# A hybrid trunk layer on one Trainium2 core: 32 of 256 tokens computed from gathered expert rows, the other 224 on the dense expert grid with both parts in one moving operand

## Chip, core and metric

The kernel runs on one core of one Trainium2 chip. A core has TensorE (matmuls, PE in the rows; PEld is its weight load), VectorE (DVE), ScalarE (ACT), GpSimd (POOL) and SyncE (SP, which issues DMAs). The metric is the device time of one execution in microseconds (us), lower is better; a median over several runs is given.

## What is computed

The input is 256 tokens of 2048 channels. The first half of the layer (a sliding-window attention, an mLSTM, a gated merge and an output projection) is untouched by the change. The second half is an expert mixer (PEER), cut here to its core:

```python
qp = (xt @ w_peer_q).reshape(T, 8, 2, 128)                 # 8 heads, two half queries
scores = einsum('thcd,hcnd->thcn', qp, peer_keys)          # against 128 keys each
s_top, i_top = top_k(scores, 16)
cand = s_top[:, :, 0, :, None] + s_top[:, :, 1, None, :]    # 16 x 16 pairs
top_s, pos = top_k(cand, 16);  idx = i0 * 128 + i1          # 16 experts of 16384, per head
gates = softmax(top_s)
act = gelu(einsum('td,thkd->thk', xb, peer_u[idx]))         # 128 rows of u per token
out = einsum('thk,thkd->td', gates * act, peer_v[idx])      # 128 rows of v per token
x = x + out
```

So a token needs 128 of the 16,384 expert rows of `peer_u` and of `peer_v` (2048 channels each).

## The kernel before

Tokens number T = 256, in NT = 2 tiles of 128; channels are 16 tiles of 128 (KT). The kernel does not gather. It streams all of `u` and all of `v` (128 blocks of 128 experts, called i) through TensorE for all tokens, and puts the gates as zeros and non-zeros into a grid `W[i]` (128 experts x 256 tokens, 128 of them; `wA` holds the first 80, `wB` the rest).

A **unit** is one `load` of 128 x 1024 fp32 weights (512 KB, SP's queue, four `raw` buffers) and its `split`: ScalarE copies `raw` to `hi` (L84, rounded to fp32r), VectorE writes `lo = raw - hi` (L85). Each product is then three fp32r matmuls: hi weights by hi and by lo of the activations, lo weights by hi. `hi` and `lo` have two buffers each. `run` prepares unit k+1, then calls `step` for unit k; `step` emits the matmuls, then the functions in `later` (those left by the unit before), then some pieces of the list `side`, as many as the pace `rate` has paid for. What stands in `side` is the work beside the stream: top-16, the lookup, the scatter.

Stages of the second half, in order:
1. `w_pq`, 32 units: query projection; `score` multiplies with the keys, `top16` runs beside it.
2. `u`, 256 units (`ws_units`): a weight block of 128 x 128 is stationary. The hi block moves 512 columns (256 tokens hi, 256 tokens lo, L158), the lo block 256 columns (L162). `total` adds the two halves of the PSUM bank, VectorE multiplies with the norm factor `rb` (L769), ScalarE applies Gelu into `W[i]`. In the first E0 = 52 blocks (104 units) top-16 over pairs (`pick16`), `lookup` (one-hot compare on VectorE, product on GpSimd L807, sum on VectorE) and `turn` run beside; in the other 76 blocks `scatter` does: for four tokens it makes one-hot rows A (VectorE) and B (ScalarE, L847 and L848), multiplies them on TensorE (L853, fp32) and multiplies the result into the blocks that are done (L862) or copies it into those that are not (L864).
3. `v`, 256 units (`v_consume`): here the grid is stationary (`ph`, `pl`, split of `W[i]`) and the weights move, 12 matmuls of 512 columns (L889, L890, L893); the 8 PSUM banks hold 2 token tiles x 2048 channels to the end. Then L904 adds the residual and stores.

The order of each engine's instructions is set by the tile scheduler when the program is built, from the order of the source and its own priorities.

Of the kernel before, what the change touches and what calls it, by code (L numbers as in the profile page):

```python
# [31 lines left out]
QU = 512  # L32


@with_exitstack
def hybrid_block_kernel(ctx: ExitStack, tc: tile.TileContext, a, out):
# [177 lines left out]
    x1d = dram.tile([T, D], F32, name="x1d")  # L214

# [145 lines left out]
    def evac_conv(n):  # L361
        def f(ps):
            total(mqk[:, n], ps)
# [240 lines left out]
    def sig(dst, ps, n):  # L604
        total(dst, ps)
# [14 lines left out]
    def evac_pA(n):  # L620
        def f(ps):
            s = wk.tile([P, T], F32, name="pa", tag="b1", bufs=NB["b1"])
            total(s, ps)
# [3 lines left out]
    def evac_pM(n):  # L627
        def f(ps):
            s = wk.tile([P, T], F32, name="pm", tag="b1", bufs=NB["b1"])
            total(s, ps)  # L630
# [39 lines left out]
    def evac_out(n):  # L670
        def f(ps):
# [15 lines left out]
            split(X2[:, n, 0], X2[:, n, 1], xg)  # L687
            later.append(lambda so=stage["o"]: turn_x1(n, x1, so))
# [13 lines left out]
    iot = exc.tile([P, P], F32, name="iot")  # L702
    G.iota(iot, pattern=[[1, P]], base=0, channel_multiplier=0, allow_small_or_imprecise_dtypes=True)
    gT = exc.tile([P, T], F32, name="gT")
    i0T = exc.tile([P, T], F32, name="i0T")
    i1T = exc.tile([P, T], F32, name="i1T")
    NA = 80
    wA = exc.tile([P, NA, T], F32, name="wA")
    eb = pool(ctx, "eb", 2)

    tks = ExitStack()
    tk = pool(tks, "tk", 1)
    keysT = tk.tile([P, 2 * PH, NK], F32, name="keysT")
# [13 lines left out]
    def score(n, q):  # L727
# [4 lines left out]
        for t in range(NT):  # L732
            side.append(lambda t=t: top16(sc[:, t, n], st_[:, t, n], it_[:, t, n]))

    def evac_q(n):
        def f(ps):
            q = eb.tile([P, T], F32, name="zu")
            total(q, ps)
            V.tensor_mul(q, q, rb)
            later.append(lambda: score(n, q))  # L740
        return f

    units = []
    for n in range(2 * PH):
        units += ws_units(a["w_pq"][n], X2, evac_q(n))
    run(units, 0.75)
    flush()
# [7 lines left out]

    def act_u(i, z):
        k = done["tok"]
        if k < T:
# [208 lines left out]
```

## Time and profile before

| | us |
|---|---|
| median of 3 runs | 2268.75 (2268.66 to 2269.9) |
| the profiled execution | 2268.72 |
| its span from first to last instruction | 2267.0 |
| TensorE busy | 2235.2 (99%) |
| VectorE busy | 1599.0 (71%) |
| ScalarE busy | 1257.8 (55%) |
| GpSimd busy | 85.9 (4%) |

The granted clock over the span is 0.999. The profiled execution lies within 0.1 us of the median, so its span plus 1.7 us outside it stands for the median. The rows below come from this execution. A busy matmul overlaps its neighbours in the records, so a matmul's real cost is read from the distance of starts, not from its duration.

### The profile page before, as it was taken

The numbers are of one execution on the slowest core, as the hardware profiler recorded it, in microseconds if no ns is written. First come the engines' busy times: TensorE is split into PE (matmuls) and PEld (weight loads), VectorE is DVE, ScalarE is ACT, GpSimd is POOL, SyncE is SP. The second block draws the span as 40 slices with busy tenths as digits, with TensorE's granted clock in tenths as the row PEclk, the third lists the DMA queues.
The fourth block names the chain that finished last, engine by engine and source line by source line (L and its number), as shares of the span: only waits on it lengthen the run. The fifth ranks groups of instructions, "written<-read, shape, count | busy, mean of one in ns | idle before, by whom it ended". The sixth has DMA issues, their size and how long they took to land.

```text
span 2267.0 us, 32407 instructions
## 1 busy us (share of the span) xinstructions
PE 2235.2 (99%) x11841; PEld 1906.3 (84%) x11841; DVE 1599.0 (71%) x2915; ACT 1257.8 (55%) x2378; POOL 85.9 (4%) x79
## 2 busy tenths in 40 slices
PE   7999999999999999999999999999999999999999
PEld 5887788888888878888888888888888888888887
DVE  7977688778889997855777788886555555555555
ACT  5755566556544444544777777775444444444443
POOL 3000000000130020200000000000000000000000
PEclk9999999999999999999999999999999999999999
DMA  6565544555665445555544444556555555555555
GB/s 204 189 191 164 169 160 160 184 186 189 211 212 188 162 164 196 181 190 186 171 165 166 165 163 167 165 170 213 195 195 193 193 194 193 194 194 193 194 192 173
DMA packets 115296, 415.66 MB, mean 183 GB/s; under 512 B 12992, under 2 KB 13120, under 8 KB 114752
## 3 DMA queue, kind: packets, MB, share of 16 engines
q1 hardware_dynamic: 115136, 413.59, 55.1%
q8 instruction: 92, 1.51, 0.3%
q14 instruction: 68, 0.56, 0.1%
HBM read 409.35 MB, written 4.19 MB: 182 GB/s over the span
## 4 chain that ended last, share of the span: by engine, by line
PE 91%; DVE 7%; ACT 1%; POOL 1%; issue 0%; DMA 0%; POOLq 0%; SPq 0%; DVEq 0%
PE mm L158 33%; PE mm L162 17%; PE sd L890 5%; PE sd L889 5%; PE mm L889 5%; PE mm L890 5%; PE sd L893 5%; PE mm L893 5%; PE sd L853 3%; DVE lo L85 2%; PE mm L184 2%; PE mm L185 2%; PE mm L189 2%; DVE oh L805 0%; DVE xg L257 0%
## 5 line engine op out<-in xcount | busy, mean ns | idle before, releaser
L85 DVE TENSOR_TENSOR lo<-raw,hi 128x1024 fp32r<-128x1024 f32 x762 | 936.5, 1229 | 611.3 <-ACT hi L84 603.4
L84 ACT ACTIVATE hi<-raw 128x1024 fp32r<-128x1024 f32 x762 | 807.0, 1059 | 863.1 <-PE mm L890 378.5
L158 PE MATMUL mm<-X,hi 128*128 128x512 f32 x3088 | 789.8, 397 | 13.8 <-ACT hi L84 8.5
L158 PEld LDWEIGHTS mm<-X,hi 128*128 128x128 f32 x3088 | 557.4, 190 | 117.7 <-ACT hi L84 8.8
L162 PEld LDWEIGHTS mm<-X,lo 128*128 128x128 f32 x3088 | 421.1, 190 | 39.7 <-DVE lo L85 9.7
L162 PE MATMUL mm<-X,lo 128*128 128x256 f32 x3088 | 433.6, 283 | 5.0 <-DVE lo L85 5.0
L889 PE MATMUL sd<-hi,ph 128*128 128x512 f32 x512 | 199.2, 389 | 0.0
L890 PE MATMUL sd<-hi,pl 128*128 128x512 f32 x512 | 199.2, 389 | 0.0
L890 PE MATMUL mm<-hi,pl 128*128 128x512 f32 x512 | 199.2, 389 | 0.0
L889 PE MATMUL mm<-hi,ph 128*128 128x512 f32 x512 | 199.2, 389 | 0.0
L893 PE MATMUL sd<-lo,ph 128*128 128x512 f32 x512 | 199.2, 389 | 0.0
L893 PE MATMUL mm<-lo,ph 128*128 128x512 f32 x512 | 199.2, 389 | 0.0
L889 PEld LDWEIGHTS mm<-hi,ph 128*128 128x128 f32 x512 | 96.1, 188 | 20.1
L893 PEld LDWEIGHTS sd<-lo,ph 128*128 128x128 f32 x512 | 96.1, 188 | 20.0
L890 PEld LDWEIGHTS mm<-hi,pl 128*128 128x128 f32 x512 | 96.1, 188 | 19.9
L889 PEld LDWEIGHTS sd<-hi,ph 128*128 128x128 f32 x512 | 96.1, 188 | 19.9
L893 PEld LDWEIGHTS mm<-lo,ph 128*128 128x128 f32 x512 | 96.1, 188 | 19.9
L890 PEld LDWEIGHTS sd<-hi,pl 128*128 128x128 f32 x512 | 96.0, 188 | 19.9
L184 PE MATMUL mm<-hi,X 128*128 128x512 f32 x224 | 89.6, 400 | 0.0
L847 ACT ACTIVATE ab<-iot,i1T 128x128 f32<-128x128 f32 x256 | 87.8, 390 | 1.4 <-DVE i1T L823 1.4
L185 PE MATMUL mm<-hi,X 128*128 128x512 f32 x224 | 88.2, 394 | 0.0
L849 DVE TENSOR_SCALAR ab<-iot,i0T,gT 128x128 f32<-128x128 f32 x256 | 74.2, 345 | 0.0
(279 smaller groups left out, 2082.4 us busy)
## 6 DMA issues: line engine op xcount, KB each, us to landing
raw<-u SPq DMA_DIRECT2D x256, 512.0 KB, 3.7
raw<-v SPq DMA_DIRECT2D x256, 512.0 KB, 3.6
raw<-w_g SPq DMA_DIRECT2D x64, 512.0 KB, 3.6
raw<-w_tok SPq DMA_DIRECT2D x56, 512.0 KB, 3.6
raw<-w_qk SPq DMA_DIRECT2D x32, 512.0 KB, 3.7
raw<-w_o SPq DMA_DIRECT2D x32, 512.0 KB, 4.0
raw<-w_pq SPq DMA_DIRECT2D x32, 512.0 KB, 3.7
raw<-w_pa SPq DMA_DIRECT2D x16, 512.0 KB, 3.5
```

The source lines that it names most:

```text
L84: S.activation(hi, src, AF.Copy)
L85: V.tensor_sub(lo, src, hi.bitcast(F32))
L158: PE.matmul(ps, hi[:, w], X[:, k].rearrange("p s t -> p (s t)"), start=(k == 0), stop=False)
L162: PE.matmul(ps[:, :T], lo[:, w], X[:, k, 0], start=False, stop=(k == kts - 1))
L184: PE.matmul(st["ps"][t], xh[:, k, ts], hi[q], start=(k == 0), stop=False)
L185: PE.matmul(st["ps"][t], xl[:, k, ts], hi[q], start=False, stop=False)
L847: S.activation(B, iot, AF.Square, bias=i1T[:, t:t + 1])
L849: V.tensor_scalar(A, iot, i0T[:, t:t + 1], gT[:, t:t + 1], op0=OP.is_equal, op1=OP.mult)
L853: PE.matmul(ps[:, j], AB[j][:, 1], AB[j][:, 0], start=True, stop=True)
L889: PE.matmul(acc[t][h * 2 + q], ph[:, ts], hi[q], start=(i == 0), stop=False)
L890: PE.matmul(acc[t][h * 2 + q], pl[:, ts], hi[q], start=False, stop=False)
L893: PE.matmul(acc[t][h * 2 + q], ph[:, ts], lo[q], start=False, stop=(i == NE - 1))
```

## The change

- **32 tokens leave the grid.** SP = 32, ND = 224: `u_units` and the scatter work on tokens 32 to 255 only. For tokens 0 to 31, `fetch` gathers by an indirect DMA on GpSimd's queue: in one fetch each of the 32 tokens gets one of its 128 expert rows, cut into four quarters of 512 channels on 4 x 32 partitions (128 x 512 fp32, 256 KB), into one of 6 `slab` buffers. `dot` (VectorE, one instruction with an accumulated sum) makes the product with x for u; `add_row` adds weight times row for v. 128 fetches and 128 dots stand in the stream of `u`, 128 fetches and 128 adds in that of `v`, paced by `rows_todo` and `row_rate`.
- **224 tokens move with parts side by side.** In `u` the moving operand is `Xn` (hi and lo of 224 tokens, 448 columns; 224 for the lo weights). `Xn` takes X2's buffer and is made between `w_pq` and `u` by `turn_to_grid` from a copy of the activations that went through DRAM (`xgd`, written from ScalarE's queue by 16 DMAs, read back in one) and was multiplied by `rb` during `w_pq`; so the multiplication per block (L769) goes.
- **The expert sum by column halves.** In `v` the weights become stationary and the grid moves: for each half of the channels, all 128 blocks, 8 matmuls of 448 columns and 8 of 224 into 8 banks; `split_w` makes hi and lo of four blocks at a time into a ring of 8 blocks, which takes `Xn`'s buffer. After each half `total` empties 8 banks. The result is channels x tokens, so `finish` turns it back by 32 transposes at the end.
- **VectorE in source order** from `w_pq` on (`manual_schedule`): the scheduler no longer reorders it. `w_pq` and `u` become one `run`; top-16 of the second token tile moves into `u`; E0 becomes 66; `pick16` looks at 112 pairs instead of 256; `lookup` takes four heads at once (8 GpSimd products of 128 x 1024 instead of 32 of 128 x 256).
- The scatter's A is one VectorE instruction for four tokens; the gate moves from A into B's second ScalarE instruction.

```diff
+SP = 32
+ND = T - SP
+PARTS = P // SP
+HD = D // PARTS
+ROW = 0.75
...
         pace[0] = min(pace[0] + rate, 4.0)
-        while pace[0] >= 1.0 and side:
-            pace[0] -= 1.0
+        if rows_todo:
+            pace[1] += row_rate[0]
+            if pace[1] >= 1.0:
+                pace[1] -= 1.0
+                pace[0] -= ROW
+                rows_todo.pop(0)()
+        while side and pace[0] >= cost(side[0]):
+            pace[0] -= cost(side[0])
             tick()
...
+            def f(parts):
+                Xn = own["Xn"]
...
+                    PE.matmul(ps[:, :2 * ND], hi[:, w], Xn[:, k].rearrange("p s t -> p (s t)"),
+                              start=(k == 0), stop=False)
...
+                    PE.matmul(ps[:, :ND], lo[:, w], Xn[:, k, 0], start=False, stop=(k == KT - 1))
...
+    def turn_to_grid():
+        own["Xn"] = xx.tile([P, KT, 2, ND], F32R, name="X")
+        for c in range(KT // 4):
+            k = slice(4 * c, 4 * c + 4)
+            split(own["Xn"][:, k, 0], own["Xn"][:, k, 1], wA[:, k])
...
+    def fetch(table, s):
+        ix = own["ix"]
+        keep(G.indirect_dma_start(out=slab[s % NSL], out_offset=None, in_=tables[table],
+                                  in_offset=bass.IndirectOffsetOnAxis(ap=ix[:, s:s + 1], axis=0)))
...
+    def dot(s):
+        sl = slab[s % NSL]
+        (V.scalar_tensor_tensor(sl, sl, 1.0, own["x"], op0=OP.mult, op1=OP.mult,
+                                    accum_out=own["dots"][:, s:s + 1]))
+        if s + NSL < NS:
+            fetch("u", s + NSL)
...
+    dve_order = tc.manual_schedule(engines={mybir.EngineType.DVE})
...
+    ue[0] = first(turn_to_grid, ue[0])
+    ue[2] = first(choose, ue[2])
+    run(units + ue, 1.0)
...
+        V.tensor_tensor(A, iot.unsqueeze(1).to_broadcast([P, TG, NK]),
+                        i0T[:, t0:t0 + TG].unsqueeze(2).to_broadcast([P, TG, NK]), op=OP.is_equal)
...
-            S.activation(B, B, AF.Relu, bias=1.0, scale=-1.0)
-            V.tensor_scalar(A, iot, i0T[:, t:t + 1], gT[:, t:t + 1], op0=OP.is_equal, op1=OP.mult)
+            S.activation(B[:, j], B[:, j], AF.Relu, bias=gT[:, t:t + 1], scale=ngT[:, t:t + 1])
...
-                PE.matmul(acc[t][h * 2 + q], ph[:, ts], hi[q], start=(i == 0), stop=False)
-                PE.matmul(acc[t][h * 2 + q], pl[:, ts], hi[q], start=False, stop=False)
...
-                PE.matmul(acc[t][h * 2 + q], ph[:, ts], lo[q], start=False, stop=(i == NE - 1))
...
+            for j in range(NB2):
+                PE.matmul(acc[h][j][:, :2 * ND], hi[:, j * P:(j + 1) * P], both, start=(i == 0), stop=False)
+            for j in range(NB2):
+                PE.matmul(acc[h][j][:, :ND], lo[:, j * P:(j + 1) * P], ring[:, i % NR, 0],
+                          start=False, stop=(i == NE - 1))
+            if i == NE - 1:
+                for j in range(NB2):
+                    total(outT[h][j], acc[h][j][:, :ND], acc[h][j][:, ND:2 * ND])
```

TensorE in the stage `v`, the second half of a unit; `sd` and `mm` are PSUM banks, and of the two names behind the arrow the first moves and the second is stationary (`hi` and `lo` are the weights, `ph` and `pl` the grid, `X` in v the ring). Before:

```order
L889 MATMUL sd<-hi,ph 128x512
L890 MATMUL sd<-hi,pl 128x512
L889 MATMUL mm<-hi,ph 128x512
L890 MATMUL mm<-hi,pl 128x512
L893 MATMUL sd<-lo,ph 128x512
L893 MATMUL mm<-lo,ph 128x512
```

TensorE in the same stage after the change, where one unit ends and the next begins:

```order
L1092 MATMUL sd<-X,lo 128x224
L1092 MATMUL mm<-X,lo 128x224
L1090 MATMUL sd<-X,hi 128x448
L1090 MATMUL mm<-X,hi 128x448
L1090 MATMUL sd<-X,hi 128x448
L1090 MATMUL mm<-X,hi 128x448
```

Twelve matmuls of 512 columns per unit became eight of 448 and eight of 224.

VectorE from `u` into `v` (`zu`, later `z`, is the sum of a block of u, `wB` the grid, `ozt` and `odots` belong to the 32 tokens, `X` is the ring). Before:

```order
L85 TENSOR_TENSOR lo<-raw,hi 128x1024
L199 TENSOR_TENSOR zu<-mm,zu 128x256
L769 TENSOR_TENSOR zu<-zu,rb 128x256
L85 TENSOR_TENSOR lo<-raw,hi 128x1024
L762 TENSOR_TENSOR wB<-wB,zu 128x256
L85 TENSOR_TENSOR lo<-raw,hi 128x1024
L85 TENSOR_TENSOR pl<-wA,ph 128x256
L85 TENSOR_TENSOR lo<-raw,hi 128x1024 x2
```

VectorE at the place where `u` ends, after the change:

```order
L90 TENSOR_TENSOR lo<-raw,hi 128x1024
L215 TENSOR_TENSOR z<-mm,z 128x224
L798 TENSOR_TENSOR wB<-wB,z 128x224
L215 TENSOR_TENSOR z<-mm,z 128x224
L798 TENSOR_TENSOR wB<-wB,z 128x224
L959 TENSOR_TENSOR ozt<-sd,rb 128x32
L961 TENSOR_TENSOR slab_6799<-ozt,gT 128x128
L966 COPY odots<-sd 128x128
L90 TENSOR_TENSOR X<-wA,X 128x4x224
L90 TENSOR_TENSOR lo<-raw,hi 128x1024 x3
```

Before, the `lo` of the first units of v stood between the last pieces of u; now the last blocks of u, the weights of the 32 tokens and the split of the first four grid blocks stand in one row ahead of the first `lo` of v.

VectorE in the scatter stage. Before (`ab` is the pair A and B, `sd` the product on TensorE):

```order
L849 TENSOR_SCALAR ab<-iot,i0T,gT 128x128 x2
L85 TENSOR_TENSOR lo<-raw,hi 128x1024 x2
L199 TENSOR_TENSOR zu<-mm,zu 128x256
L769 TENSOR_TENSOR zu<-zu,rb 128x256
L85 TENSOR_TENSOR lo<-raw,hi 128x1024
L762 TENSOR_TENSOR wB<-wB,zu 128x144
L862 TENSOR_TENSOR wA<-sd,wA 128x4x80
L849 TENSOR_SCALAR ab<-iot,i0T,gT 128x128 x4
```

VectorE in the scatter stage after the change (L949 is the `dot` of a gathered slab):

```order
L90 TENSOR_TENSOR lo<-raw,hi 128x1024
L798 TENSOR_TENSOR wB<-wB,z 128x88
L949 SCALAR_TENSOR_TENSOR slab_6801,odots<-slab_6801,ox 128x512
L1040 TENSOR_TENSOR wA<-sd,wA 128x80x4
L1040 TENSOR_TENSOR wB<-sd,wB 128x9x4
L1040 TENSOR_TENSOR wA<-sd,wA 128x80x4
L1040 TENSOR_TENSOR wB<-sd,wB 128x9x4
L90 TENSOR_TENSOR lo<-raw,hi 128x1024
L215 TENSOR_TENSOR z<-mm,z 128x224
```

The dots of the gathered rows came in, the multiplication by `rb` and the four single A rows went out, and the products into the grid follow each other.

## Rows read from the trace of the kernel before

**Rows 1.** The page: busy time and share, and the chain that ended last by line.
```profile
PE 2235.2 (99%) x11841; PEld 1906.3 (84%) x11841; DVE 1599.0 (71%) x2915; ACT 1257.8 (55%) x2378; POOL 85.9 (4%) x79
...
PE mm L158 33%; PE mm L162 17%; PE sd L890 5%; PE sd L889 5%; PE mm L889 5%; PE mm L890 5%; PE sd L893 5%; PE mm L893 5%; PE sd L853 3%; DVE lo L85 2%; PE mm L184 2%; PE mm L185 2%; PE mm L189 2%; DVE oh L805 0%; DVE xg L257 0%
```

**Rows 2.** Busy time by stage: w_pq, u with lookup, u with scatter, v.
```profile
core 0: us, PE busy (x) PEld busy (x) DVE busy (x) ACT busy (x) POOL busy (x), PEclk, DMA share, GB/s
692.00:774.00 82.00, 80.35 (x465) 69.01 (x464) 80.41 (x311) 36.19 (x52) 0.00 (x0) 1.00 0.48 161
774.00:1065.00 291.00, 285.47 (x1623) 247.43 (x1622) 221.72 (x437) 146.51 (x224) 36.51 (x32) 1.00 0.55 183
1065.00:1557.00 492.00, 492.00 (x3004) 439.39 (x3003) 382.39 (x738) 359.36 (x972) 0.00 (x0) 1.00 0.50 166
1557.00:2261.00 704.00, 704.00 (x3119) 583.35 (x3118) 362.83 (x394) 312.00 (x387) 0.00 (x0) 1.00 0.59 194
```

**Rows 3.** Timeline of TensorE in u: start, length, line, count (merged).
```profile
1063.40 2.00 PE L158 MATMUL mm<-X,hi 128*128 128x512 f32 x8
1065.24 1.11 PE L162 MATMUL mm<-X,lo 128*128 128x256 f32 x8
1066.19 2.00 PE L158 MATMUL mm<-X,hi 128*128 128x512 f32 x8
```

**Rows 4.** Timeline of TensorE in v: two starts ten matmuls apart.
```profile
1567.60 0.39 PE L893 MATMUL mm<-lo,ph 128*128 128x512 f32 x1
...
1569.87 0.39 PE L893 MATMUL mm<-lo,ph 128*128 128x512 f32 x1
```

**Rows 5.** Timeline of TensorE in the scatter: eight matmuls of four tokens.
```profile
1322.12 1.05 PE L853 MATMUL sd<-ab 128*128 128x128 f32 x8
```

**Rows 6.** Groups of weight loads, 128 and 64 columns, and L853: count, busy us, mean ns.
```profile
L162 PEld LDWEIGHTS mm<-X,lo 128*128 128x128 f32 x3088 | 421.1, 190 | 39.7 <-DVE lo L85 9.7
...
L853 PE MATMUL sd<-ab 128*128 128x128 f32 x512 | 66.3, 275 | 0.0
...
L518 PEld LDWEIGHTS sd<-pT,av 128*64 128x64 f32 x48 | 2.4, 134 | 3.9 <-issue 3.7 <-ACT hi L84 0.2
```

**Rows 7.** Groups of VectorE and ScalarE, whole span, by shape: busy us, mean ns.
```profile
L85 DVE TENSOR_TENSOR lo<-raw,hi 128x1024 fp32r<-128x1024 f32 x762 | 936.5, 1229 | 611.3 <-ACT hi L84 603.4 <-PE sd L853 4.5 <-ACT sr L78 0.6
L84 ACT ACTIVATE hi<-raw 128x1024 fp32r<-128x1024 f32 x762 | 807.0, 1059 | 863.1 <-PE mm L890 378.5 <-PE mm L158 277.4 <-issue 126.9
...
L199 DVE TENSOR_TENSOR zu<-mm,zu 128x256 f32<-128x256 f32 x144 | 60.1, 418 | 0.0
...
L198 ACT ACTIVATE zu<-mm 128x256 f32<-128x256 f32 x144 | 53.3, 370 | 0.2 <-PE mm L162 0.2
...
L862 DVE TENSOR_TENSOR wA<-sd,wA 128x320 f32<-128x320 f32 x40 | 36.1, 902 | 0.0
...
L487 DVE SCALAR_TENSOR_TENSOR s<-sd,msk 128x512 f32<-128x512 f32 x8 | 5.1, 684 | 0.0
```

**Rows 8.** GpSimd's product L807 by its line: min/median/max ns, first and last start.
```profile
L807 POOL TENSOR_TENSOR oh<-oh,itf x32: 727/927/1739, 801.7 to 943.0; 128x256 f32<-128x256 f32 x32
```

**Rows 9.** Timeline of all engines, two products of GpSimd beside VectorE's lo.
```profile
870.28 2.46 POOL L807 TENSOR_TENSOR oh<-oh,itf 128x256 f32<-128x256 f32 x2 [0.42 <-DVE oh L805]
...
870.40 1.75 DVE L85 TENSOR_TENSOR lo<-raw,hi 128x1024 fp32r<-128x1024 f32 x1
```

**Rows 10.** Timeline of all engines, the end of the program.
```profile
2261.20 0.39 PE L893 MATMUL mm<-lo,ph 128*128 128x512 f32 x1
...
2262.16 0.68 DVE L904 TENSOR_TENSOR X<-sd,X 128x512 f32<-128x512 f32 x1
2262.75 0.68 DVE L904 TENSOR_TENSOR X<-mm,X 128x512 f32<-128x512 f32 x1
```

**Rows 11.** DMA issues: KB each, median us to landing.
```profile
raw<-u SPq DMA_DIRECT2D x256, 512.0 KB, 3.7
...
out<-X SPq DMA_DIRECT2D x8, 256.0 KB, 2.3
```

More of the change, by code (lines that the diff above doesn't have):

```diff
@@ L732, in score, with g @@
         for t in range(NT):
-            side.append(lambda t=t: top16(sc[:, t, n], st_[:, t, n], it_[:, t, n]))
+            (side, second)[t].append((1.7, lambda t=t: top16(sc[:, t, n], st_[:, t, n], it_[:, t, n])))
     def evac_q(n):
-        def f(ps):
-            q = eb.tile([P, T], F32, name="zu")
-            total(q, ps)
+        def g(ps):
+            q = eb.tile([P, T], F32, name="z")
+            total(q, ps[:, :T], ps[:, T:])
             V.tensor_mul(q, q, rb)
             later.append(lambda: score(n, q))
[L741 to L747, printed above, removed]
+        return lambda ps: later.append(lambda: g(ps))
     W = [wA, None]
@@ new lines, in own_index, with own_rows @@
+    def own_index():
+        V.tensor_mul(own["x"], own["x"], slab[NSL - 1])
+        ef = tk.tile([SP, NS], F32, name="ef")
+        V.scalar_tensor_tensor(ef, iv[0:SP, 0], float(NK), iv[0:SP, 1], op0=OP.mult, op1=OP.add)
+        G.dma_start(exd, ef)
+        for c in range(PARTS):
+            G.dma_start(own["ixf"][c * SP:(c + 1) * SP], exd)
+    def own_rows():
+        V.tensor_scalar(own["ixf"], own["ixf"], float(PARTS), part, op0=OP.mult, op1=OP.add)
+        V.tensor_copy(own["ix"], own["ixf"])
+        for s in range(NSL):
+            fetch("u", s)
+        rows_todo.extend([lambda s=s: dot(s) for s in range(NS)])
@@ new lines, in dot, with own_weights @@
+    def dot(s):
[4 more added lines that the diff above has]
+            fetch("u", s + NSL)
+    def own_weights():
+        zt, wt, wgt = own["zt"], slab[0][:, 0:NS], own["dots"]
+        zp = psd.tile([P, QU], F32, name="sd")
+        PE.matmul(zp[:, 0:SP], own["dots"], pair, start=True, stop=True)
+        yield
+        V.tensor_mul(zt, zp[:, 0:SP], rb[:, 0:SP])
+        S.activation(zt, zt, AF.Gelu)
+        V.tensor_mul(wt.rearrange("p (c t) -> p c t", c=PARTS), zt.unsqueeze(1).to_broadcast([P, PARTS, SP]),
+                     gT[:, 0:SP].unsqueeze(1).to_broadcast([P, PARTS, SP]))
+        yield
+        wp = psd.tile([P, QU], F32, name="sd")
+        PE.transpose(wp[:, 0:NS], wt, ident)
+        V.tensor_copy(wgt, wp[:, 0:NS])
+        for s in range(NSL):
+            fetch("v", s)
@@ new lines, in hybrid_block_kernel @@
+    run(u_units(E0, NE), (ROW * len(rows_todo) + 2.1 * len(side)) / left)
+    drain()
+    while rows_todo:
+        rows_todo.pop(0)()
+    NB2 = HU // P
+    NR = 8
+    EG = 4
+    ring = xx.tile([P, NR, 2, ND], F32R, name="X")
+    flat = wA.rearrange("p i t -> p (i t)")
+    x1 = flat[:, 0:2 * D].rearrange("p (t d) -> p t d", d=D)
+    x1s = flat[:, 2 * D:2 * D + HD]
+    n0 = P - SP
+    oT = [eb.tile([P, 2, ND], F32, name="oT", tag="AB"[j % 2]) for j in range(NB2 // 2)]
+    t0 = 2 * D + HD
@@ L900, in hybrid_block_kernel @@
+    units[NE + 40] = first(load_x1, units[NE + 40])
+    units[-3] = first(own_out, units[-3])
     run(units)
+    flush()
+    assert not rows_todo
     for q in range(4):
[L902 to L905 removed]
+        finish(q)
+    dve_order.__exit__(None, None, None)
 def kernel(**inputs):
```

270 lines of the change are left out of this document (189 added, 81 removed).

## The prediction, made before the changed kernel was run

> **What bounds the kernel now.** I read the page first: TensorE is busy for 99% of the span, and the chain that ended last runs through its matmuls of the streamed weights, L158, L162 and L889 to L893 [rows 1]. Then the busy time by stage: TensorE has no idle time in the scatter part of `u` and in `v`, and loses 5.5 us of 291 in the lookup part; VectorE is at 78% in the scatter part and 52% in `v`, ScalarE at 73% and 44%, the clock is at its upper level (1.00 of 2.4 GHz) everywhere and the DMA engines are busy to 0.50 to 0.59 [rows 2]. So what counts is TensorE's time per unit, and after the change whether the engines beside it still keep up. That time is read from starts, since records of matmuls overlap.
>
> A unit of `u` repeats after 1066.19 - 1063.40 = 2.79 us: eight matmuls of 512 columns in 1.84 (0.230 each), eight of 256 in 0.95 (0.119 each) [rows 3]. In `v` ten matmuls of 512 take 1569.87 - 1567.60 = 2.27, so 0.227 each and 2.72 for the twelve of a unit [rows 4].
>
> **Fewer columns.** Between 256 and 512 columns the price rises by (0.230 - 0.119)/256 = 0.434 ns per column. So 448 columns cost 0.230 - 64 x 0.434 ns = 0.202 in `u` and 0.227 - 0.028 = 0.199 in `v`. For 224 columns the same line gives 0.105. But each of these matmuls brings its own 128 x 128 weights. A load of 128 columns lasts 190 ns, one of 64 columns 134 [rows 6]: 56 ns per 64 columns, 112 per 128. And where matmuls of only 128 columns follow each other with new weights, in the scatter, eight take 1.05 us with 0.275 for one [rows 5, 6]: (1.05 - 0.275)/7 = 0.111 from start to start. No stream with full weights here is faster, so I take 0.111. The bounds are 0.105 (the line) and 0.119 (256 columns, the nearest shape of this number type: the floor is already reached there). Unit of `u` afterwards: 8 x 0.202 + 8 x 0.111 = 2.50, 0.29 less, times 256: -73 us. Unit of `v`: 8 x 0.199 + 8 x 0.111 = 2.48, 0.24 less, times 256: -61 us. At 0.105 both together gain 25 us more (4096 matmuls x 6 ns), at 0.119 33 us less.
>
> The Trainium skill ("TensorE: Matmul & The Clock Gate", LDWEIGHTS) speaks against the full saving: a load takes its columns divided by 1.2 in ns, 107 for 128 columns, whatever moves. The loads of 64 and 128 columns above agree (112). By it the small matmul costs at least 0.107, an estimate, and the sum below would be 16 us lower than with 0.111.
>
> **Fewer tokens in the scatter.** The chain has 3% on L853 [rows 1]. Per token there are two matmuls at 0.111; 32 tokens less give -7 us.
>
> **What takes new time on the path.** Five places, in each of which TensorE waits for something that stands in VectorE's fixed order.
> (1) `w_pq` to `u`: `Xn` takes X2's buffer, so its split can start only after the last matmul of `w_pq`. Four ScalarE copies and four VectorE subtractions of 896 elements, by the 1024-element rows 0.93 and 1.08 each [rows 7]. The first group is there after 2.1 us, the four after 5.3, then `total`, the multiplication and the next `lo` (0.4 + 0.4 + 1.2) come behind them in source order: unit two gets its lo at about 7.2 instead of 4.1. TensorE uses the waiting for the matmuls of the first groups; I put the loss at +3.4.
> (2) From lookup to scatter the stream is emptied: the first `lo` stands behind the last `total`: +0.5.
> (3) `u` to `v`: copy 0.35, add 0.39, Gelu 0.37, multiply 0.39 (the 256-element rows 370 and 418 cut to 224 [rows 7]), then three small VectorE steps (0.2 to 0.3 each), a Gelu and a transpose between them (0.6 with the hand-overs), then the split of the ring, 1.1; some 0.7 for crossing engines. Together 4.7, with nothing of v that TensorE could do: +4.8. The scheduler had put `lo` of v between these before.
> (4) Middle of `v`: eight banks are emptied at 0.39 each while the next half wants one bank every 0.2: +1.7.
> (5) The end: before, from the last matmul's start at 2261.20 to 2267.0 [rows 10]. After: eight `total` (3.3), then eight adds of 512 elements, whose starts lie 0.6 apart [rows 10], beside 32 transposes, then the last store (256 KB, 2.3 to land [rows 11]): about 12.1 after the last matmul instead of 5.4: +6.7.
> Sum: +17 us.
>
> **What lies beside the stream.** VectorE in the scatter part, 62 blocks or 124 units: TensorE needs 124 x 2.50 + 56 x 0.89 = 360 us. VectorE: 124 `lo` x 1.229 = 152; 56 A of 512 elements x 0.69 = 38; 56 products into the grid, between 0.65 (contiguous, by the slope of the other rows) and 1.13 (0.902 for 320 elements with the old stride, plus the rest) = 36 to 63; 79 dots x 0.75 = 59 (0.684 for a three-operand instruction of 512 elements, plus something for the sum it writes); 62 `total` x 0.39 = 24; 62 multiplications x 0.28 = 17. In all 326 to 353 of 360 [rows 7]. Lengths overlap (0.68 long, 0.60 apart [rows 10]), so some 290 to 315 really: 80 to 87%, as much as before plus a little. ScalarE: 359 us before, of which 152 x 1.059 = 161 are `hi`; now 124 x 1.059 = 131 and the other 198 times 0.85 = 168, so 299 of 360, 83% [rows 2, 7]. Neither becomes the bound by its sum; that VectorE now waits in a fixed order costs something. In the lookup part GpSimd has 8 products four times as long: alone the old one takes 727 ns, beside VectorE up to 1739, and VectorE's `lo` then takes 1.75 instead of 1.23 [rows 8, 9]. A product of 1024 elements (about 2.6 alone) can hold a `lo` up to that long, against a slack of one `lo` buffer, about 2.8 us. I take +8 for all this, bounds 0 and +40 (a tenth of the part with the scatter).
>
> The Trainium skill ("SBUF — State Buffer", SBUF: two separate sides) has the rule for this: VectorE with two SBUF inputs and GpSimd reading SBUF share one port pair, and the later one waits for the other's whole instruction. The 1.75 agrees.
>
> **The gathers.** No row of the trace shows an indirect DMA. Data: 256 KB every 4.4 to 5 us beside 512 KB every 2.5, so (0.51 + 0.06 MB per us) 260 GB/s at most; the DMA engines moved 194 at a share of 0.59 [rows 2], so about 0.8: a weight load will land later than 3.7 us [rows 11], with four buffers for it. Six slabs give a fetch about 25 us. Only the start (index to DRAM, back, first six fetches) is a chain that VectorE waits in: by the store's 2.3 us [rows 11] three hops make 7, against five units of distance: +2, bounds 0 and +8. The 16 stores of `xgd`, its load and the multiplication by `rb` lie in `w_o` and `w_pq` beside TensorE; VectorE in `w_pq` loses the second tile's top-16, which covers it. If that cover failed, the 4 x 1.08 would show as waits in `w_pq`. The multiplication L769 and the 24 GpSimd instructions that go were hidden: nothing.
>
> **Sum.** -73 - 61 - 7 + 17 + 8 + 2 = -114 us against the profiled execution's own 2268.7, which is the median too: **2154 us**.
>
> **Rivals.** (a) The floor of the weights is 0.119, not 0.111: 2187 us. For it: the nearest shape of fp32r shows just that; against it: the scatter's 0.111. (b) VectorE, in order, falls behind in lookup and scatter: the dots and A instructions stand ahead of `lo`, and each product into the grid waits for TensorE. Loss up to 40 and the gain of the small matmul partly given back: about 2205 us. (c) Slower: the matmuls of 224 columns run at the price of plain fp32. Every fp32r matmul of the trace has 256 or 512 columns, so none shows what fewer do. Plain fp32 pays two matmuls of 0.111 for 128 columns [rows 5], 0.39 for 224: 4096 x 0.28 = +1145 us, 3300 us. It decides from 0.139 on, where the 114 us are used up. (d) Slower: GpSimd needs longer per fetch than the 4.4 to 5 us between them; then 256 fetches set the time, and beyond 5.1 us each the gain is gone (at 8 us, +650). The nearest issues, from SP, take far less. (e) That the 32 tokens don't leave the stream is excluded by the order: 448 and 224 columns stand there.
>
> **Chances.** Forecast with pitch 0.105 to 0.111 and light waits 0.50; (a) 0.17; (b) 0.18; (c) 0.07; (d) 0.04; gains eaten by waits to within 0.2%, about what a measurement can tell from no change, 0.02; the rest just above it 0.02. So faster 0.85, same 0.02, slower 0.13. The range reaches from the line's 0.105 with no loss beside the stream (2121) to (b) with its upper end near 2225; (c) and (d) stay outside.
>
> **What would show it.** Starts of L1092 0.111 apart and a period of 2.50 in `u`, 2.48 in `v`; no idle TensorE within `v` except 1.7 in its middle; a gap of 5 us at the end of `u`, and 12 us behind the last matmul. Wrong if L1092 follows at 0.119 or 0.39, if TensorE waits for `lo` in the lookup or scatter part by more than 20 us, or if VectorE waits for slabs.

## The result, and the profile after

The changed kernel takes 2232.9 us (median; 2231.9 to 2233.0) where the kernel before took 2269.2 (its median with a fourth run): ratio 0.984, 95% interval 0.982 to 0.986. The sign of the forecast holds, its size does not: 36 us instead of 115, and 2232.9 lies above the range's end of 2225. The profiled execution's span is 2230.1 us.

Its page: busy time of TensorE, its clock in 40 slices, and GpSimd's gathers with their waiting.

```profile
PE 2132.3 (96%) x12836; PEld 1938.7 (87%) x12836; DVE 1689.4 (76%) x2905; ACT 1283.9 (58%) x2238; POOL 389.7 (17%) x324
...
PEclk9999999999998999999999999999999999999999
...
L919 POOL DMA_INDIRECT slab<-ur,oix x128 | 162.6, 1270 | 452.9 <-DVE slab L949 431.6
```

TensorE was busy for 99% of a longer span before [rows 1]; now 96%. The price per unit came out as forecast. TensorE's timeline in the quiet middle of `u`, where [rows 3] stood, and in `v`, where [rows 4] stood:

```profile
1004.16 1.79 PE L818 MATMUL mm<-X,hi 128*128 128x448 f32 x8
1005.79 1.05 PE L823 MATMUL mm<-X,lo 128*128 128x224 f32 x8
1006.68 1.59 PE L818 MATMUL mm<-X,hi 128*128 128x448 f32 x7
```

```profile
1600.40 0.38 PE L1090 MATMUL sd<-X,hi 128*128 128x448 f32 x1
...
1602.91 0.38 PE L1090 MATMUL sd<-X,hi 128*128 128x448 f32 x1
```

In `u` eight of 448 columns take 1.63, eight of 224 take 0.89 (0.204 and 0.111 each): a step (the matmuls of one unit) of 2.52 in these rows, 2.51 in the median of the lookup part. In `v` a step is 1602.91 - 1600.40 = 2.51, after 2.72. The loss is elsewhere. Busy time by stage (`w_pq`; `u` with lookup; `u` with scatter; `v`), to be read against [rows 2]:

```profile
700.00:799.00 99.00, 90.83 (x532) 80.53 (x532) 76.81 (x188) 44.94 (x64) 0.00 (x0) 0.95 0.48 165
799.00:1161.00 362.00, 343.52 (x2122) 319.09 (x2123) 301.64 (x648) 183.15 (x286) 110.00 (x68) 0.99 0.68 230
1161.00:1566.00 405.00, 377.80 (x2433) 356.61 (x2433) 292.19 (x557) 322.90 (x807) 76.96 (x73) 0.97 0.62 210
1571.00:2218.00 647.00, 645.93 (x4096) 614.95 (x4096) 462.45 (x458) 325.23 (x328) 149.63 (x127) 1.00 0.78 261
```

`v` has next to no idle TensorE. At 2.51 a step the lookup part needs 132 x 2.51 = 331 us and takes 362. The scatter part needs 124 x 2.51 + 56 groups x 8 x 0.112 = 361 and takes 405. The granted clock, 1.00 in all four stages before, is at 0.95, 0.99 and 0.97 in the three stages with waits.

`w_pq` ends late. The first matmuls of `u`, before and after:

```profile
783.28 2.00 PE L158 MATMUL mm<-X,hi 128*128 128x512 f32 x8
```

```profile
799.03 3.33 PE L818 MATMUL mm<-X,hi 128*128 128x448 f32 x8 [4.97 <-DVE X L90]
```

(The windows of [rows 2] begin 8 to 18 us ahead of their stages: in the kernel before the first unit with scatter begins at 1083.0, the first of `v` at 1565.1.) From the first matmul of each stage, in us, beside the terms of the prediction's sum (for `u` -73 - 7 + 0.5 + 4.8 + 8 + 2, for `v` -61 + 1.7):

| | before | after | change | forecast |
|---|---|---|---|---|
| up to `u` | 783.3 | 799.0 | +15.7 | +3.4 |
| `u` | 781.8 | 772.1 | -9.7 | -65 |
| `v`, to its last matmul's start | 696.1 | 646.8 | -49.3 | -59 |
| from there to the end | 5.8 | 12.2 | +6.4 | +6.7 |

So `u` misses its forecast by 55 us, the way to it by 12, and `v` by 10.

TensorE's waits over the whole span (us in total, times, longest):

```profile
PE mm L818 <- ACT hi L89: 21.4, 33, 2.1
PE sd L1029 <- DVE A L1020: 15.0, 7, 3.9
PE mm L178 <- DVE lo L90: 13.7, 1, 13.7
PE mm L823 <- DVE lo L90: 9.1, 11, 1.4
```

The single wait of 13.7 us is in `w_pq`. All engines there:

```profile
689.69 0.33 SPq L739 DMA_DIRECT2D wA<-xgd  x1
...
698.95 3.10 DVE L743 TENSOR_TENSOR wA<-wA,rb 128x896 f32<-128x896 f32 x3 [9.85 <-DMA wA<-xgd]
701.96 1.22 DVE L90 TENSOR_TENSOR lo<-raw,hi 128x1024 fp32r<-128x1024 f32 x1
...
703.21 0.33 SPq L94 DMA_DIRECT2D raw<-w_pq  x1
```

VectorE stands at L743 for 9.85 us, until the load of `xgd` lands; three of its multiplications follow, and only then the `lo` that TensorE wants. Since that `lo` also gives `raw` back, the next weight load on SP is issued at 703.21. This is the cover that the prediction took for granted.

The waits for `hi` and for A are one chain, here in the scatter part around 1285 us:

```profile
1284.57 0.49 ACT L1025 ACTIVATE B<-B,gT,ngT 128x128 f32<-128x128 f32 x1
1284.97 1.04 ACT L89 ACTIVATE hi<-raw 128x1024 fp32r<-128x1024 f32 x1
...
1286.04 1.23 DVE L90 TENSOR_TENSOR lo<-raw,hi 128x1024 fp32r<-128x1024 f32 x1 [2.03 <-ACT hi L89]
...
1287.18 0.38 DVE L215 TENSOR_TENSOR z<-mm,z 128x224 f32<-128x224 f32 x1
1287.48 1.28 DVE L1020 TENSOR_TENSOR A<-ones,i0T 128x512 f32<-128x512 f32 x2
...
1288.22 2.08 PE L1029 MATMUL sd<-A,B 128*128 128x128 f32 x8 [3.01 <-DVE A L1020]
...
1289.95 2.40 PE L818 MATMUL mm<-X,hi 128*128 128x448 f32 x8
```

ScalarE makes B ahead of `hi`; `hi` is late, so VectorE's `lo` is late, and in source order `z` and A stand behind it; TensorE waits 3.01 us for A. Behind the wait the eight scatter matmuls last 2.08 us instead of 1.05 [rows 5]: they run at the lower of the two clock levels. TensorE in that stretch (length, busy and instructions; the granted clock is the 0.50):

```profile
1288.20:1290.30 2.10, 2.08 (x9) 0.50 0.69 250
```

The waits for `lo` stand nearly all in the lookup part (8.6 us), and 7.6 us of them beside GpSimd's products of `lookup`, each of them now 128 x 1024:

```profile
1098.93 2.40 POOL L878 TENSOR_TENSOR oh<-oh,itf 128x1024 f32<-128x1024 f32 x1 [0.70 <-DVE oh L875]
1099.12 3.29 DVE L90 TENSOR_TENSOR lo<-raw,hi 128x1024 fp32r<-128x1024 f32 x1 [0.28 <-ACT hi L89]
...
1102.46 1.15 PE L823 MATMUL mm<-X,lo 128*128 128x224 f32 x8 [1.14 <-DVE lo L90]
```

This `lo` takes 3.29 us instead of 1.22 and ends 1.08 us behind the product; seven of the 130 in the part last 1.6 to 3.3 us, 11.8 us more in all.

### The profile page after: what moved, and what is told of

It is laid out like the page before. It is cut to its first block, busy times and chain, and to the rows that moved or that the text cites. A ratio compares the mean times of both kernels' runs of the same rounds, so it can differ in the third digit from the quotient of the medians.

```text
span 2230.1 us, 35017 instructions
## 1 busy us (share of the span) xinstructions
PE 2132.3 (96%) x12836; PEld 1938.7 (87%) x12836; DVE 1689.4 (76%) x2905; ACT 1283.9 (58%) x2238; POOL 389.7 (17%) x324
## 5 line engine op out<-in xcount | busy, mean ns | idle before, releaser
L818 PE MATMUL mm<-X,hi 128*128 128x448 f32 x2048 | 473.2, 374 | 26.5 <-ACT hi L89 21.4
L818 PEld LDWEIGHTS mm<-X,hi 128*128 128x128 f32 x2048 | 370.8, 191 | 57.7 <-ACT hi L89 28.3
L1090 PE MATMUL sd<-X,hi 128*128 128x448 f32 x1024 | 377.2, 368 | 2.5 <-DVE X L90 1.5
L1090 PE MATMUL mm<-X,hi 128*128 128x448 f32 x1024 | 375.5, 367 | 0.0
L174 PE MATMUL mm<-X,hi 128*128 128x512 f32 x1040 | 272.5, 403 | 15.4 <-ACT hi L89 8.7
L823 PEld LDWEIGHTS mm<-X,lo 128*128 128x128 f32 x2048 | 268.0, 192 | 22.1 <-DVE lo L90 15.3
L823 PE MATMUL mm<-X,lo 128*128 128x224 f32 x2048 | 270.8, 275 | 9.1 <-DVE lo L90 9.1
L1092 PE MATMUL mm<-X,lo 128*128 128x224 f32 x1024 | 241.5, 274 | 0.0
L1092 PE MATMUL sd<-X,lo 128*128 128x224 f32 x1024 | 239.7, 272 | 0.0
L174 PEld LDWEIGHTS mm<-X,hi 128*128 128x128 f32 x1040 | 190.4, 192 | 53.6 <-ACT hi L89 9.1
L1090 PEld LDWEIGHTS sd<-X,hi 128*128 128x128 f32 x1024 | 193.9, 189 | 13.8 <-issue 1.7
L1090 PEld LDWEIGHTS mm<-X,hi 128*128 128x128 f32 x1024 | 193.9, 189 | 13.2
L1092 PEld LDWEIGHTS sd<-X,lo 128*128 128x128 f32 x1024 | 195.6, 191 | 3.8
L1092 PEld LDWEIGHTS mm<-X,lo 128*128 128x128 f32 x1024 | 195.7, 191 | 2.8
L178 PEld LDWEIGHTS mm<-X,lo 128*128 128x128 f32 x1040 | 143.3, 192 | 24.5 <-DVE lo L90 14.1
L178 PE MATMUL mm<-X,lo 128*128 128x256 f32 x1040 | 147.1, 284 | 13.7 <-DVE lo L90 13.7
```

Of the source, the lines that this page charges most:

```text
L174: PE.matmul(ps, hi[:, w], X[:, k].rearrange("p s t -> p (s t)"), start=(k == 0), stop=False)
L178: PE.matmul(ps[:, :T], lo[:, w], X[:, k, 0], start=False, stop=(k == kts - 1))
L818: PE.matmul(ps[:, :2 * ND], hi[:, w], Xn[:, k].rearrange("p s t -> p (s t)"), start=(k == 0), stop=False)
L823: PE.matmul(ps[:, :ND], lo[:, w], Xn[:, k, 0], start=False, stop=(k == KT - 1))
L1090: PE.matmul(acc[h][j][:, :2 * ND], hi[:, j * P:(j + 1) * P], both, start=(i == 0), stop=False)
L1092: PE.matmul(acc[h][j][:, :ND], lo[:, j * P:(j + 1) * P], ring[:, i % NR, 0], start=False, stop=(i == NE - 1))
```

## The experiments

All kernels are edits of the changed one (2232.9 us). Theory W, tried first, is on `w_pq`; S, V and L are on `u`: ScalarE too slow, VectorE too slow, or the two waiting for one another. Times of parts are from the profiled execution: first matmul of `u`, of its step 132, and of `v` (so the scatter part, 410 us in the changed kernel, holds the 5 us between `u` and `v`); between builds the first of them moves by up to 2.6 us with no edit ahead of it.

**1. The norm later in `w_pq`.**

```diff
-    side += [(0.1, load_xg)] + [(1.0, lambda c=c: norm_xg(c)) for c in range(KT // 4)]
+    side += [(0.1, load_xg)]
...
+        if n % 2 == 0 and 4 <= n <= 10:
+            side.append((1.0, lambda: norm_xg(n // 2 - 2)))
```

> One edit: the four multiplications of the 224 columns by the norm (L743) leave the front of VectorE's order in w_pq and stand one each behind the scores of n = 4, 6, 8 and 10; the load that they wait for stays where it is. Theory W (VectorE's fixed order makes lo, and so TensorE, wait for that load and these four, and the clock falls behind the wait): the wait of TensorE of 13.7 us for lo at 690 us goes, u begins at 778 to 783 us instead of 799, and the whole falls by 15 to 21 us, to 2212 to 2218 us. Rival D (the load itself, 1.8 MB in the same queue as the weights, is what holds w_pq up): the weights are late behind it all the same, u begins at 790 us or later and the whole falls by under 9 us.

Measured 2203.7 us (ratio to before 0.971, 0.969 to 0.973), 29 less. TensorE's waits now, for the row of 13.7 us in `w_pq` 1.3 us:

```profile
PE mm L820 <- ACT hi L89: 24.2, 43, 1.7
...
PE sd L1031 <- DVE A L1022: 4.9, 7, 1.2
```

`u` begins at 784.6, 14.4 earlier: theory W, without its last few us; the load itself stayed, so rival D falls. The other 14 us came where nothing was edited: lookup part 357.9 (-4), scatter part 400.3 (-10), with waits for A of 4.9 instead of 15.0. 80 dots are left for the scatter part instead of 79, which changes the rate by which its pieces are dealt out to steps. That this shift is the cause was only argued; it shows that the waits for A hang on which pieces meet in one step.

**2. The gate back into A.**

```diff
-            S.activation(B[:, j], B[:, j], AF.Relu, bias=gT[:, t:t + 1], scale=ngT[:, t:t + 1])
+            S.activation(B[:, j], B[:, j], AF.Relu, bias=1.0, scale=-1.0)
+            V.tensor_scalar(A[:, j], iot, i0T[:, t:t + 1], gT[:, t:t + 1], op0=OP.is_equal, op1=OP.mult)
```

> One edit in the scatter: ScalarE's Relu takes the constants 1 and -1 again and the gate goes back into A, made by four multiplications-with-compare per group of four tokens on VectorE instead of one compare; that takes about 4 x 0.19 = 0.75 us per group off ScalarE (56 groups: 42 us) and adds 4 x 0.34 - 0.69 = 0.69 us per group to VectorE (38 us). Theory S (in the scatter part, 1161 to 1566 us, ScalarE is the late one: hi comes late, and VectorE's order passes that on): the part falls by 15 to 40 us. Theory V (VectorE, in its fixed order, is the late one, and A is late behind its own work): the part grows by 10 to 40 us. Under theory L (the two engines wait for one another in a loop, of which the Gelu that waits for z is the link) little changes, within 8 us.

Measured 2218.4 us (0.978, 0.976 to 0.979); the scatter part 399.3, 11 less. VectorE got 20 us more work there and ScalarE 36 us less, and it became faster: V as the sole cause falls. The gain, net of what VectorE took over, is under S's 15 and above L's 8, and waits for `hi` (8.9) and A (8.9) remain.

**3. The Gelu one step later.**

```diff
-        later.append(lambda: act_u(i, z))
+        later.append(lambda: later.append(lambda: act_u(i, z)))
```

> One edit: the Gelu of a unit of u and its product are issued one step later than now, so that ScalarE does not stand before hi waiting for VectorE's z. Theory L: ScalarE's wait for z (58 us in the scatter part, 25 us between 800 and 860 us) goes nearly to nothing, hi is on time, the stretches of 2.61 and 3.46 us per step go, and the whole falls by 25 to 55 us, to 2180 to 2208 us. Theory S (too much work on ScalarE in the scatter part): the stretch 800 to 960 us gains up to 20 us and the scatter part under 10. Theory V (VectorE's own work is ahead of lo and A): under 8 us in all.

Measured 2228.0 us (0.982, 0.980 to 0.984), 5 less. It tried nothing: ScalarE's order is the scheduler's, and it put the Gelu back to its old place: z, Gelu, `hi`, `hi` in 63 of 66 blocks, as in the changed kernel. Run 9 tries it.

**4. No rows in `u`.**

```diff
-        for s in range(NSL):
-            fetch("u", s)
-        rows_todo.extend([lambda s=s: dot(s) for s in range(NS)])
+        V.memset(own["dots"], 0.0)
```

> Left out: the 128 gathered slabs of u and their dot products (the dots are set to zero, so the peer part of the first 32 tokens is missing); the gathers and sums of v stay. With them go 128 x 0.77 us of VectorE, 49 of them before 1161 us and 79 behind, and the gathers' bytes beside u. Theory V: the scatter part loses VectorE's 61 us of 405 and the waits for A, and falls by 20 us or more. Theories S and L: under 10 us in the scatter part. That the gathers take the weights' bandwidth: hi waits for raw, and both parts gain; it would show as ScalarE waiting less for raw where nothing else stands before it.

Measured 2211.8 us (0.975, 0.973 to 0.976). The lookup part stays (360.6), the scatter part falls by 17 to 393.1. TensorE's waits in it, first the one for `hi` in the changed kernel (all 15.0 us for A fall into this part too), then those of this run:

```profile
PE mm L818 <- ACT hi L89: 11.6, 18, 1.4
```

```profile
PE mm L818 <- ACT hi L89: 16.7, 22, 1.8
...
PE sd L1027 <- DVE A L1018: 0.6, 1, 0.6
```

So the waits for A go with the dots ahead of it, as V has it, though 17 us is short of V's 20. But `hi` is no less late without them: 27 of the 44 us lost in this part, and all but 1.4 of the 31 of the lookup part, are neither theirs nor the gathers' bytes'.

**5. VectorE out of source order.**

```diff
-    dve_order = tc.manual_schedule(engines={mybir.EngineType.DVE})
-    dve_order.__enter__()
...
-    dve_order.__exit__(None, None, None)
```

> One part of the change undone: VectorE's instructions from w_pq on go in the scheduler's order again instead of source order. Theory O (the fixed order is what costs: in it VectorE stands at L743 for a load in w_pq, and at lo for hi elsewhere while other work is ready): w_pq gets back 12 to 15 us, the lookup and the scatter parts 10 to 25 us, the whole falls to 2195 to 2212 us. Rival Q (the order brought as much as it cost: without it the dots, the choosing and A crowd in front of lo and z): w_pq gets back 12 to 15 us but u grows by as much or more, and the whole is within 8 us of 2232.9 us or above.

Measured 2463.1 us (1.086, 1.084 to 1.087): 230 slower than the change, 193 slower than before. `w_pq` got its 14 us back (`u` begins at 785.4), and the rest is Q, far beyond what was expected. Its waits, and its stages lookup and `v`:

```profile
PE mm L823 <- DVE lo L90: 74.6, 24, 5.7
PE sd L1090 <- DVE lo L90: 59.3, 19, 5.9
```

```profile
785.00:1288.00 503.00, 394.57 (x2120) 359.79 (x2121) 320.70 (x634) 187.69 (x286) 164.37 (x141) 0.84 0.63 204
...
1682.00:2443.00 761.00, 685.42 (x4089) 639.16 (x4090) 470.43 (x458) 325.35 (x325) 146.91 (x128) 0.93 0.68 221
```

The scheduler moves all 128 dots of `u` into the lookup part and puts other work ahead of `lo` there and in `v`; the clock falls to 0.84 and 0.93. With the rows in, the order is worth 230 us, a part that the prediction had not priced.

**6. B in two places.**

```diff
         for j in range(TG):
+            if j == TG // 2:
+                yield
...
-    side += [(0.7, scatter(t0)) for t0 in range(SP, T, TG)]
+    side += [(0.525, scatter(t0)) for t0 in range(SP, T, TG)]
```

> One edit in the scatter: B of a group of four tokens is made in two places of the order, two tokens each, so that ScalarE has at most 1.75 us of it at a time before hi and not 3.5 us, and A stands one place further ahead of its matmul; the work and its mean pace (2.1 per group) stay. Theory S1 (it is the lump of 3.5 us ahead of hi that makes hi late): the waits for hi fall, the waits for A (15 us) go nearly to nothing, and the scatter part falls by 20 us or more from 410 us. Theory S2 (it is ScalarE's total there, 79% of the time): hi waits as before and the part falls by the waits for A alone, 8 to 15 us. If it is the place of A alone, the waits for A go and those for hi stay.

Measured 2217.2 us (0.977, 0.975 to 0.979); the scatter part 395.5, 15 less, as much as the waits for A, which go from 15.0 to 1.8, while those for `hi` there stay (14.8 after 11.6). It was A's place. Of the lump of B the run says nothing: ScalarE's order is the scheduler's, and 34 of 70 stretches between two `hi` hold 3 us of B or more, where in the changed kernel 32 of 74 do. So S1 was not tried.

**7 and 10. A third `hi`, and its control.** To make room, four slabs instead of six; run 10 has the four slabs alone.

```diff
-        hi = strm.tile([P, HU], F32R, name="hi", bufs=2)
+        hi = strm.tile([P, HU], F32R, name="hi", bufs=3)
...
-    NSL = 6
+    NSL = 4
```

> Two sizes: three buffers for hi instead of two, and four slabs for gathered rows instead of six to make room. ScalarE can make hi one step earlier (2.5 us), if it has the time. If hi is late because it waits for a free buffer (the matmuls of two steps before, L818), the lookup part falls by 8 to 18 us (of its 18 us of gaps and 10 us of slow clock) and the scatter part by 5 to 20 us. If hi is late because ScalarE is behind in its own order, little changes, under 6 us in all. If four slabs are too few, the wait of the dots for a slab (1.7 us, once) grows to many.

> The control for the run with three hi: only the four slabs for gathered rows in place of six, hi with two buffers. If the gain of 45 us there was the third hi's: 2230 to 2240 us here. If it was the slabs' (fewer gathers in flight, or other places in memory): 2200 us or below.

Measured 2188.2 us (0.964, 0.963 to 0.966) with the third `hi`, 2232.2 with the slabs alone: the 45 us are the buffer's. Lookup 347.4 (-15), scatter 386.2 (-24); `u` begins 6 earlier, most of it won ahead of `w_pq` (3.2 us against run 10), in the half of the layer that the change leaves alone. No wait for `hi` is left in `u`. ScalarE's timeline in the lookup part, of the changed kernel and of this one, and last of the kernel before:

```profile
1001.98 0.34 ACT L214 ACTIVATE z<-mm 128x224 f32<-128x224 f32 x1
1005.17 0.39 ACT L795 ACTIVATE wA<-z 128x224 f32<-128x224 f32 x1 [2.85 <-DVE z L215]
1005.47 1.99 ACT L89 ACTIVATE hi<-raw 128x1024 fp32r<-128x1024 f32 x2
```

```profile
1005.00 0.34 ACT L214 ACTIVATE z<-mm 128x224 f32<-128x224 f32 x1
1006.48 0.39 ACT L795 ACTIVATE wA<-z 128x224 f32<-128x224 f32 x1 [1.15 <-DVE z L215]
1007.34 1.06 ACT L89 ACTIVATE hi<-raw 128x1024 fp32r<-128x1024 f32 x1 [0.47 <-PE mm L823]
```

```profile
1004.66 0.37 ACT L198 ACTIVATE zu<-mm 128x256 f32<-128x256 f32 x1
1006.44 1.06 ACT L84 ACTIVATE hi<-raw 128x1024 fp32r<-128x1024 f32 x1 [1.41 <-PE mm L158]
1007.41 0.40 ACT L759 ACTIVATE wA<-zu 128x256 f32<-128x256 f32 x1
```

In the changed kernel ScalarE stands 2.85 us before the Gelu, and both next `hi` come behind it; the first ends at 1006.5, just when TensorE wants it (1006.68 above). The third buffer doesn't change this order; it lets each `hi` be made a step earlier, so that a stand of 1 to 3 us no longer reaches TensorE. In the kernel before one `hi` stood between z and the Gelu (in 48 of 52 blocks of the lookup part): the order that puts both behind the Gelu (in 63 of 66) came in with the change. ScalarE's order is the scheduler's in both kernels.

**9. ScalarE in source order.**

```diff
-    dve_order = tc.manual_schedule(engines={mybir.EngineType.DVE})
+    dve_order = tc.manual_schedule(engines={mybir.EngineType.DVE, mybir.EngineType.Activation})
```

> One edit: ScalarE is put in source order as VectorE is, where now the scheduler sets its order; in the third run the Gelu that was issued a step later still stood in the same place of ScalarE's order (z, Gelu, hi, hi), so that run did not try theory L. In source order the next hi stands ahead of the Gelu that waits for VectorE's z. Theory L (ScalarE's stand before that Gelu, 154 us in the lookup part and 58 us in the scatter part, is what makes hi late): the lookup part falls by 10 us or more from 362 us, the scatter part by 10 us or more from 410 us, the whole to 2180 to 2210 us. Rival B (hi is late since it has only two buffers, with whatever order): the lookup part stays within 5 us, and source order puts the scatter's B in lumps, so that the whole is 2225 us or above.

Measured 2309.2 us (1.017, 1.016 to 1.019), slower than before. ScalarE's order in the lookup part is now z, `hi`, Gelu, `hi`, as before the change; then TensorE's waits for `hi` in the scatter part, and ScalarE's own largest there:

```profile
1003.25 0.34 ACT L214 ACTIVATE z<-mm 128x224 f32<-128x224 f32 x1
1004.74 1.06 ACT L89 ACTIVATE hi<-raw 128x1024 fp32r<-128x1024 f32 x1 [1.16 <-PE mm L818]
1005.71 0.37 ACT L795 ACTIVATE wA<-z 128x224 f32<-128x224 f32 x1
```

```profile
PE mm L818 <- ACT hi L89: 59.2, 41, 3.7
```

```profile
ACT wB L1042 <- DVE wB L1040: 74.1, 36, 3.3
```

The two parts answer differently. In the lookup part L holds: the stand before the Gelu is gone, the waits for `hi` fall from 9.8 to 2.3 us, and the part to 352.0 (-10). In the scatter part waits for `hi` rise to 59 us and the part to 498 us. Rival B forecast the total, by lumps of B (4 x (0.39 + 0.485) = 3.5 us) ahead of `hi`, and they are there. But there is more: ScalarE now stands before its copies of the scatter's product into the grid (L1042), which wait for VectorE's product into the same grid (L1040), with the next `hi` behind them: 74.1 us and, for `wA`, another 25.1, where both together were 4.8 in the changed kernel. Run 11 sets the two apart.

**8, 11 and 12. Together.** Run 8 has edits 1, 2, 6 and 7; run 11 those and source order on ScalarE; run 12 edits 1, 2 and 6, with two `hi` and six slabs.

> All of it together: the norm's multiplications later (as in the first run), the gate in A (second run), B in two places, three hi and four slabs. If the gains add up: 2232.9 - 29 - 14 - 15 for B and A, and up to 15 for hi, so 2160 to 2180 us. If they are gains on the same gaps (each makes the same hi less late), 2185 to 2198 us. If something else holds the scatter part (VectorE's total, 77%, with A dearer by 0.69 us a group), it stays at 395 us or above and the whole above 2195 us.

> The version with all edits (2159.8 us: norm later, gate in A, B in two places, three hi, four slabs), and ScalarE in source order as well. Under L another 5 to 12 us of its lookup part (344.6 us, of which 331 is the matmuls alone) and scatter part (372.0 us, 361 alone) go: 2148 to 2155 us. Under B it is the same within 3 us or dearer.

> The version with all edits but with two hi and six slabs again: what the third hi is worth once the order and the lumps are mended. If the third hi and the edits fill the same gaps: 2165 to 2178 us, so that the third hi is worth 5 to 18 us there. If they add up: 2195 to 2208 us, as the third hi alone brought 45 us.

Measured: 2159.8 us (0.952, 0.950 to 0.953) for run 8, 2227.9 (0.982, 0.980 to 0.983) for run 11, 2194.9 (0.968, 0.966 to 0.969) for run 12. So the third `hi` is worth 35 us on top of the other edits. The gains do not add up: singly the edits bring 29, 14, 16 and 45, which is 104, and together 73; edits 1, 2 and 6 bring 59 singly and 38 together. They fill in part the same gaps. That run 8 lands at the edge of the range given for gains that add up is luck: the third `hi` alone brought 45, where that range had up to 15 for it. Source order on ScalarE brings nothing once `hi` has a third buffer (lookup 346.7 after 344.6) and costs 67 us in the scatter part. The lumps are not what costs there: with edits 2 and 6 only 6 of 73 stretches between two `hi` hold 3 us of B or more (in run 9 all 44), but ScalarE stands before the copies for 96.5 us, as in run 9, and TensorE waits 42.3 us for `hi`. So run 9's total fits rival B's range by another way than B gave. Run 8 beats both kernels; its stages:

```profile
782.00:1126.00 344.00, 338.42 (x2120) 319.26 (x2120) 300.12 (x646) 183.65 (x286) 106.33 (x65) 0.99 0.72 240
1126.00:1493.00 367.00, 363.96 (x2436) 347.70 (x2435) 312.51 (x728) 283.71 (x808) 79.34 (x76) 1.00 0.72 233
```

Where the matmuls alone need 331 us the lookup part takes 344, and where they need 361 the scatter part takes 367: with most of the waits mended the version is near the forecast for the change (2154). Some 4 us come from the third `hi` ahead of `w_pq` (its first matmul is at 675.2, in run 12 at 679.0), and whether a third `hi` would help the kernel before was not tried; in its `u` TensorE waited 5.0 us for `lo` and never for `hi`.

## Why the prediction was right and wrong

- **Fewer columns: right in `u`, a little small in `v`.** 0.203 and 0.111 were forecast as 0.202 and 0.111; in `v` 0.203 instead of 0.199, so 2.51 instead of 2.48 a step, 8 us. Rival (a) falls, and (c): the 224 columns run at 0.111, not 0.39. The Trainium skill ("TensorE: Matmul & The Clock Gate", LDWEIGHTS) gives 0.107 for the load; the matmuls of 224 and of 128 columns both stand at 0.111 to 0.112, a little above its figure. That the weight load sets this floor fits these rows, but no run tried it apart.
- **New waits on the path: right.** `w_pq` to `u` 5.0 (forecast 3.4); `u` to `v` 2.8 + 1.5 = 4.4 (4.8); middle of `v` 0.9 (1.7); from the last matmul to the end 12 (12.1).
- **The gathers: right.** VectorE waited for a slab once, 1.7 us; GpSimd took 1.27 us a fetch and mostly waited for VectorE. Rival (d) falls. The DMA engines moved 261 GB/s at a share of 0.78 in `v`; the 260 and 0.8 of the prediction hold, though the 0.51 MB per us that it adds up from should be 0.21 (512 KB in 2.5 us).
- **"VectorE in `w_pq` loses the second tile's top-16, which covers it": wrong**, 14 us. The prediction counted VectorE's free time in `w_pq`, but in a fixed order it matters where the wait stands, not how much time is free. The wait stood ahead of a `lo`. The prediction even gave the size of the multiplications, 4 x 1.08, as what would show a failed cover, and left out the 9.85 us until the load lands.
- **"I take +8 for all this, bounds 0 and +40": wrong**, and the bound too. Against the matmuls alone the lookup part lost 31 us and the scatter part 44, 75 together; the kernel before, counted the same way, lost about 10 in `u`. Three edits each took a part of it away: the third `hi` 39 of its 45 (the rest ahead of `u`), A further ahead of its matmul and so no longer late behind the dots 15, ScalarE's cheaper Relu 11. They overlap, as run 12 shows, so they are not shares of the 75. What the prediction did name there, `lo` held up by GpSimd's longer products, came and by itself made 7.6 us of waits, about the whole +8; no run took it away. Rival (b) had the mechanism but put its price at 2205 us, and only for VectorE; that ScalarE stands for VectorE's `z`, VectorE for ScalarE's `hi`, and TensorE for both, was in no rival. The test by sums (VectorE 80 to 87%, ScalarE 83%) said that both keep up; the trace has them at 72 and 80% of the scatter part and late all the same. The prediction's own sign for this, more than 20 us of waits for `lo`, did not show: TensorE waited 9.1 us for `lo` there, but 21.4 for `hi` and 15.0 for A, which it had not named.
- **The clock after waits** was left out. At 0.97 over 405 us up to 12 us are lost there, at 0.95 over 99 us up to 5 (estimates, and upper bounds: the clock is also low in the waits themselves).
- **Source order** was entered as a cost ("something"). Run 5 shows it as worth 230 us.

Open: what makes `hi` late in the scatter part with two buffers and the scheduler's order: B ahead of it, ScalarE's total, or the stand before the Gelu, 58 us there. Run 6 left B's places nearly as they were, and run 9 put another wait in. In the kernel before, four tokens' B stood together between two `hi` nearly everywhere (46 of 62 places), at 2.79 us a step and with the cheaper Relu, and TensorE didn't wait for `hi`. B off ScalarE altogether was not tried. Open too is why the scheduler gave ScalarE another order after the change.

## What to carry to other kernels

When a step on the critical engine becomes 10% shorter, check the rings between the engines (the buffers that one fills and another empties) and not only their busy shares: two `hi` buffers were enough at 2.79 us a step, with one `hi` ahead of the Gelu, and were worth 45 us less than three at 2.51. Read the order of the engines that the scheduler still sets as well: here it had put both `hi` behind a Gelu that waits for VectorE, and one `hi` ahead of it again took the waits for `hi` in the lookup part from 9.8 to 2.3 us. In a hand-set order, an instruction that waits for a DMA goes behind the work that the critical engine wants next. Source order helps only where nothing in it waits ahead of what the critical engine wants: ScalarE in it cost 76 us here, as it stood for VectorE before its copies; VectorE in it gained 230. And don't add up gains that were measured one at a time.

## What the runs showed of the hardware

A Relu whose scale and bias are pointers (values read from a tile, one per partition) takes ScalarE 485 ns where constants take 298, at the same 128 elements: 224 x 0.187 = 42 us of work that the prediction, which scaled ScalarE's old time by the tokens, had not seen. In the changed kernel, then in run 2:

```profile
L1025 ACT ACTIVATE B<-B,gT,ngT 128x128 f32<-128x128 f32 x224 | 102.4, 485 | 0.7
```

```profile
L1023 ACT ACTIVATE B<-B x224: 292/298/315, 890.1 to 1520.2; 128x128 f32<-128x128 f32 x112
```

The Trainium skill ("ScalarE: Activation LUTs", What ACT_TABLE_LOAD costs) has this as 93 ns for each pointer operand, so 186 for two; the rows agree.

A wait cost more than its length: TensorE stood for 3.01 us up to 1288.22, the granted clock behind it was at the lower level (0.50 from 1288.20 to 1290.30, shown with the result), and the next two groups of eight matmuls took 2.08 and 2.40 us, where such eights take 1.05 and 1.79.
